# Attention scores as three 64-row products a head, gate arithmetic held behind attention, and higher ranks for evacuations and mLSTM steps

## The chip, the cores and the metric

One of the eight cores of a Trainium2 chip runs the whole program. The metric is the device time of one execution in microseconds (us), the median of several runs. The engines are TensorE (in the rows: PE for products, PEld for weight loads), VectorE (DVE), ScalarE (ACT), GpSimd (POOL) and SyncE (SP, which issues the DMAs).

## The reference

Two layers of a hybrid decoder over 1040 positions (16 learned meta tokens and 1024 inputs) of width 1024. Each layer normalizes its input, projects it once to 6408 columns, runs two groups of heads on the result, gates them, and projects back.

```
def hybrid_layer(x, ...):
    h = rms_norm(x, norm_g)
    z = h @ w_in
    aq, ak, av, ag, mq, mk, mv, mi, mf, mo, mgate = split(z)
    q, k = partial_rope(rms_norm(aq)), partial_rope(rms_norm(ak))     # 16 heads of 64, 2 kv heads
    ya = sliding_window_sink_attention(q, k, av, sink) * silu(ag)     # window 128, 16 meta keys, a sink
    qk = silu(causal_depthwise_conv([mq, mk]))                        # 4 mLSTM heads of 128
    hm = mlstm_chunkwise(mq, mk, mv, mi + b_i, log_sigmoid(mf + b_f)) # values of 256
    ym = rms_norm(hm) * sigmoid(mo) * silu(mgate)
    return x + concat(ya, ym) @ w_out
```

In attention, `scores = q k^T`; a query sees the meta keys, the keys of its window and a sink logit.

## The kernel before, in words

All arithmetic is float32. A matrix product is made of parts: each operand is split into a high part `hi`, rounded to the type that TensorE takes in one pass, and the rest `lo = x - hi`. A product is then `hi hi + hi lo + lo hi`, three passes into one PSUM bank. ScalarE makes `hi` (a copy), VectorE or GpSimd `lo` (a subtraction).

The 1040 positions stand as nine tiles, `TT`: one of 16 and eight of 128. A layer has these stages: keys and values; then attention; then the mLSTM; then the output projection (`pss`, `pj`, `po` at L1169).

**Attention.** Heads go in eight pairs `j`. For each pair and block `b` (nine blocks in the first layer, eight in the second, 136 steps in all) four tasks run: `s1` makes the scores of both heads in the two banks of a tile `S` and the softmax; `s2` transposes the probabilities into `T`, and evacuates them as `hi` and `lo` (L707 to L711); `s3` and `s4` multiply with the values into `O` and evacuate (L742, L744). `step(i)` emits `s1` of step i, `s2` of step i-2, `s3` and `s4` of step i-3. `weave` puts projections for coming stages between the steps, by parts of a few products (`projT_parts`, `projN_parts`, L224). TensorE's instructions keep the order of the program here (`pin`, while `in_order[0]` holds).

For the scores, `q_stacks` transposes a half pair of queries into a bank, and `q_put` splits it: for each head the 64 rows of `hi` and the 64 rows of `lo` stand one above the other in 128 rows. `Ks[0]` and `Ks[1]` hold `hi` and `lo` of the keys, each twice, in rows 0 to 63 and 64 to 127. So one product of 128 rows with `Ks[0]` gives `hi hi + lo hi`, a second with `Ks[1]` the rest: two products a head, four a step, of 272 columns (144 in the first full block of a pair, 16 in the block of the meta tokens).

**After attention** the TensorE order is free again, and the banks are given out anew. `gates` (L762 and on) computes the mLSTM's gate rows for all heads, first with Abs, Exp and Ln on ScalarE (L767 to L769); Ln needs a load of another function table. Its transposes (L772, L773) write a bank that attention used. Convolutions (`conv_tasks`, L854 to L862) run beside.

**The mLSTM.** For each of four heads `m_tasks` gives 27 steps and more: `sa(c)` prepares chunk `c` (splits of values and keys at L916, L917, L922, L923, products by `mm_split` at L904), `sb(c)` computes its result, `sc_(c)` transposes it. They are woven with projections for values (`v_tasks`), convolutions and output gates (`mo_tasks`).

Outside the pinned stretches, and for all engines but TensorE inside them, the order of an engine's instructions comes from a planner that replays the program with its own costs and takes the ready instruction of best rank first. The rank is the place in the program; `tc.high_priority(offset=EARLY)` moves it 80 places ahead, and -EARLY back. `tc.issue_after(x)` keeps instructions behind `x` on `x`'s engine. Weights come in by SP's DMAs, and are split into a ring of eight pairs by ScalarE (L158) and GpSimd (L159).

Of the kernel before, what the change touches and what calls it, by code (L numbers as in the profile page):

```python
# [15 lines left out]
ALU = mybir.AluOpType  # L16
# [46 lines left out]
def build(ctx, tc, I, O):  # L63
# [298 lines left out]
    for l in range(DEPTH):  # L362
# [9 lines left out]
        VR = unit()[:, :].rearrange("p (t c) -> p t c", t=9)  # L372
        KT = unit()[:, :].rearrange("p (a c) -> p a c", a=8)
        SS = []
        blk = [0, 0]

        def k_chain(kg, ta, tb):
# [214 lines left out]
            return [lambda i=i: st["post", half][i]() for i in range(4)]  # L592

        def q_put(Q, ps, n):
            Q = Q.rearrange("p (h c) -> p h c", h=2)
            sc.activation(Q[0:64, 0], ps[0:64, 0:n], AF.Copy)
            sc.activation(Q[64:128, 1], ps[64:128, 0:n], AF.Copy)
            ve.tensor_tensor(Q[64:128, 0], ps[0:64, 0:n], Q[0:64, 0], op=ALU.subtract)
            ve.tensor_tensor(Q[0:64, 1], ps[64:128, 0:n], Q[64:128, 1], op=ALU.subtract)  # L599

        def q_unit(j, g):
            if ("Q", g) not in A[j]:
# [46 lines left out]
        def att_tasks(j, st):  # L649
# [3 lines left out]
            def s1(b):  # L653
                t0, p = TT[b]
                S = SS[blk[0] % 2]
                blk[0] += 1
                k0, kn, o = (0, 16, 128) if b == 0 else (0, 144, 128) if b == 1 else (16 + (b - 2) * 144, 272, 0)
                for h in range(2):
                    U = st["Q", b > 4]
                    i = (b - 1) % 4  # L660
                    lq = U[:, 1024 + 16 * h:1040 + 16 * h] if b == 0 else U[:, 512 * h + 128 * i:512 * h + 128 * i + 128]
                    for i in range(2):
                        pin(pe.matmul(S[:p, h, o + 2 - 2 * h:o + 2 - 2 * h + kn], lq, Ks[i][:, k0:k0 + kn],
                                  start=(i == 0), stop=(i == 1)))
                if st.setdefault("S", 0) < 2:
                    ve.tensor_copy(cols(S, 1, 783, 1), snk[:, l, 2 * j:2 * j + 2].rearrange("p (h c) -> p h c", c=1))
                st["S"] += 1
                band = cols(S, 2, 654, 128)
                if b == 0:
                    ve.memset(band[:p], NEG)  # L670
                    mk = mask[:p, 128:144].bitcast(U32).rearrange("p (a c) -> p a c", a=1).to_broadcast([p, 2, 16])
                    ve.copy_predicated(cols(S, 130, 510, 16)[:p], mk,
                                       neg[:p].rearrange("p (a c) -> p a c", a=1).to_broadcast([p, 2, 16]))
                else:
                    if b == 1:
                        ve.memset(cols(S, 2, 510, 128), NEG)
                    ve.copy_predicated(band, mask.bitcast(U32).rearrange("p (h c) -> p h c", h=2),
                                       cols(S, 146, 366, 128))
                mx = sm.tile([128, 3, 2], F32, name="mx", bufs=4)
                P = tp_.tile([128, 384], F32, name="t")  # L680
                ve.tensor_reduce(mx[:p, 0], cols(S, 1, 639, 145)[:p], axis=mybir.AxisListType.X, op=ALU.max,  # L681
                                 negate=True)
                for h in range(2):
                    sc.activation(P[:p, 145 * h:145 * h + 145], S[:p, h, 1 + 127 * h:146 + 127 * h], AF.Exp,  # L684
                                  bias=mx[:p, 0, h:h + 1], accum_out=mx[:p, 1, h:h + 1])
                ve.reciprocal(mx[:p, 2], mx[:p, 1])  # L686
                for h in range(2):
                    Pn = P[:p, 1 + 144 * h:145 + 144 * h]
                    sc.activation(Pn, Pn, AF.Copy, scale=mx[:p, 2, h:h + 1])  # L689
                live[b] = P  # L690
# [39 lines left out]
            def s4(b):  # L730

                t0, p = TT[b]
                pm, OW, O = live.pop(b)
                G = st["G"]
                prods = [(VM[:, kv, h, :], pm[:, 0:p], O[:, p * h:p * h + p]) for h in range(2)]
                if b > 1:
                    prods += [(DV[:, b - 2], OW[:, c:c + 256], O) for c in (0, 256)]
                for i, (V, R, o) in enumerate(prods):
                    pin(pe.matmul(o, V, R, start=(b == 0), stop=(b == 0 or i == len(prods) - 1)))
                up, y = w1k(), w1k()  # L740
                with tc.high_priority(offset=EARLY):
                    sc.activation(up[0:64, 0:2 * p], O[64:128, 0:2 * p], AF.Copy)  # L742
                    for h in range(2):
                        ve.tensor_tensor(y[64 * h:64 * h + 64, :p], O[0:64, p * h:p * h + p],  # L744
                                         up[0:64, p * h:p * h + p], op=ALU.add)
                    if "QM" in st:
                        q_put(q_unit(j + 1, 0)[:, 1024:1056], st.pop("QM"), 16)
                gp.tensor_tensor(G[:, t0:t0 + p], G[:, t0:t0 + p], y[:, 0:p], op=ALU.mult)  # L748
                for t0, n, tiles in CH:
                    if b == tiles[-1]:  # L750
                        a = N_META if (t0 == 0 and last) else t0
                        sy.dma_start(spool[j, :, a:t0 + n], G[:, a:t0 + n])
# [9 lines left out]
        def gates(GR):  # L762
# [1 line left out]
            li = GT[:, 0].rearrange("p t h -> p (t h)")  # L764
            e = sm.tile([128, NR], F32, name="ge")
            lf = sm.tile([128, NR], F32, name="glf")
            sc.activation(e, zf, AF.Abs)  # L767
            sc.activation(e, e, AF.Exp, scale=-1.0)
            sc.activation(e, e, AF.Ln, bias=1.0)  # L769
            ve.scalar_tensor_tensor(lf, zf, 0.0, e, ALU.min, ALU.subtract)  # L770
# [51 lines left out]
        def v_tasks(h, wgf, st):  # L822
            def tile_task(t):
                p = TT[t][1]
                if t == 0:
                    v_units(st)
                ps = projN(wgf(), t, 256)
                sc.activation(st["V"](t)[:p, 0:256], ps[:p, 0:256], AF.Copy)
            return [lambda t=t: tile_task(t) for t in range(9)]

        def v_parts(h, wgf, st):
# [11 lines left out]
        def conv_tasks(h, wgf, st):  # L843
            def chunk_task(which, c):
# [6 lines left out]
                out, RAW = st["qk"[which]], st["raw"]  # L851
                t0, n, _ = CH[c]
                ps = projT(wgf(), 128 * which, t0, n)
                sc.activation(RAW[:, 3 + t0:3 + t0 + n], ps[:, :n], AF.Copy)  # L854
                z = t384(n)
                ve.tensor_scalar(z, RAW[:, t0:t0 + n], wcol(0), cw[:, l, 32 + tj:33 + tj],
                                 ALU.mult, ALU.add)
# [7 lines left out]
        def mo_tasks(u, wgf, st, held=None):  # L865
            def chunk_task(c):
                a, n, _ = CH[c]
                e = a + n
                a = N_META if (c == 0 and last) else a
                n = e - a  # L870
                ps = projT(wgf(), 0, a, n)
                t1 = t384(n)
                sc.activation(t1, ps[:, :n], AF.Tanh, scale=0.5)  # L873
                ps = projT(wgf(), 128, a, n)
                t2 = t384(n)
                sc.activation(t2, ps[:, :n], AF.Tanh, scale=0.5)  # L876
                ve.scalar_tensor_tensor(t2, t2, 1.0, ps[:, :n], ALU.add, ALU.mult)  # L877
                if held is None:
                    ve.scalar_tensor_tensor(t1, t1, 1.0, t2, ALU.add, ALU.mult)
                    gate_store(8 + u, st["Y"][u % 2], t1, a, e)  # L880
                    return
                if c == 0:
                    st["G", u] = unit()
                t3 = st["G", u][:, a:e]
                ve.scalar_tensor_tensor(t3, t1, 1.0, t2, ALU.add, ALU.mult)
                held.append(lambda: gate_store(8 + u, st["Y"][u % 2], t3, a, e))
            return [lambda c=c: chunk_task(c) for c in range(3)]

        def m_tasks(h, st):
# [11 lines left out]

            def mm_split(out, a, b):
                for i, (x, y) in enumerate(((a[0], b[0]), (a[0], b[1]), (a[1], b[0]))):
                    pin(pe.matmul(out, x, y, start=(i == 0), stop=(i == 2)))  # L904

            def sa(c):
                t0, p = TT[c]
# [9 lines left out]
                gp.tensor_tensor(V[1], v, V[0], op=ALU.subtract)  # L917
                if c < 8:
                    pk = bank("pt")
                    pin(pe.transpose(pk[:p, 0:128], kc, ident))  # L920
                    kt = KQ[:p, 0:128], KQ[:p, 128:256]
                    sc.activation(kt[0], pk[:p, 0:128], AF.Copy, scale=TK[:p, 2, r:r + 1])  # L922
                    ve.scalar_tensor_tensor(kt[1], pk[:p, 0:128], TK[:p, 2, r:r + 1], kt[0],  # L923
# [13 lines left out]
                De = w1k()  # L937
                sc.activation(De[:p, :p], st["EB"][:p, c, :p], AF.Exp, bias=TK[:p, 3, r:r + 1])
                pS = bank("pss")
                pin(pe.matmul(pS[:p, :p], kc, qc, start=True, stop=True))  # L940
                ve.tensor_tensor(De[:p, :p], pS[:p, :p], De[:p, :p], op=ALU.mult)
                DR = w1k(F32R)
                dr_ = DR[:p, 0:p], DR[:p, 128:128 + p]
# [39 lines left out]
            def sc_(c):  # L983
# [3 lines left out]
                hs = live.pop(c)  # L987
                ph = bank("pt")
                for f in range(2):
                    pin(pe.transpose(ph[:, 128 * f:128 * f + p], hs[:p, 128 * f:128 * f + 128], ident[:p, :p]))  # L990
                for f in range(2):
                    u = 2 * h + f
                    sc.activation(st["Y"][f][:, t0:t0 + p], ph[:, 128 * f:128 * f + p], AF.Copy,
                                  scale=cw[:, l, 40 + u:41 + u])

            out = [begin]
            for c in range(11):
                if c < 9:
                    out.append(lambda c=c: sa(c))
                if 0 <= c - 1 < 9:  # L1000
                    out.append(lambda c=c - 1: sb(c))
                if 0 <= c - 2 < 9:
                    out.append(lambda c=c - 2: sc_(c))
            return out


# [262 lines left out]
```

## Time and profile before

| what | value |
|---|---|
| median of 3 runs | 1961.46 us (1961.37 to 1962.85) |
| the profiled execution, its own time | 1962.62 us |
| its span, first to last instruction | 1960.9 us |
| TensorE products, busy | 1912.5 us (98%) |
| TensorE weight loads, busy | 1801.3 us (92%) |
| VectorE, ScalarE, GpSimd, busy | 1095.6, 1062.0, 915.8 us |
| mean granted TensorE clock | 0.997 of full speed |

Busy time of TensorE runs from a product's issue to its modelled end, and products overlap in the pipeline: what one product adds to a dense stream is the distance from its start to the next start. Layer 1 has its attention from about 76 to 415 us and its mLSTM to about 815; layer 2 from about 1045 to 1384 and to 1775.

### The profile page before, as it was taken

What the parts mean: (1) busy time and instruction counts of PE and PEld (TensorE: products, weight loads), DVE (VectorE), ACT (ScalarE), POOL (GpSimd) and SP (SyncE); (2) the same over time, 40 slices, a digit from 0 to 9 for tenths busy, and PEclk for the clock granted to TensorE, in tenths of its full rate; (3) what the DMA queues carried; (4) which work ended last, traced back from release to release, by engine and by line L of the source; (5) the groups of instructions that cost most, each with busy time, mean ns of one, the idle gap of its engine ahead of it and who ended that gap; (6) DMA issues with size and microseconds to landing.
All of it is one profiled execution on the core that took longest, in us unless ns stands there. A gap on an engine that the chain in (4) does not pass through costs nothing. (4 is left out here: it accounts for less than half of the span.)

```text
span 1960.9 us, 36174 instructions
## 1 busy us (share of the span) xinstructions
PE 1912.5 (98%) x12827; PEld 1801.3 (92%) x12827; DVE 1095.6 (56%) x2962; ACT 1062.0 (54%) x3133; POOL 915.8 (47%) x1106
## 2 busy tenths in 40 slices
PE   8999999999999999999999999999999999999999
PEld 7998998989999999877889999999999999998787
DVE  7777777667445363432446678776673635436211
ACT  6677777746454544643334677777364535446221
POOL 3544544336545454654335345443364454646342
PEclk9999999999999999999999999999999999999999
DMA  4111111121222121454541111112122121216543
GB/s 152 44 37 51 39 40 34 36 64 38 58 58 60 41 56 56 147 180 153 170 132 49 40 36 54 43 37 59 39 59 63 40 67 49 57 52 193 170 143 128
DMA packets 150838, 148.28 MB, mean 76 GB/s; under 512 B 15081, under 2 KB 123921, under 8 KB 150658
## 3 DMA queue, kind: packets, MB, share of 16 engines
q1 hardware_dynamic: 150658, 145.97, 25.5%
q8 instruction: 101, 1.65, 0.4%
q14 instruction: 79, 0.65, 0.1%
HBM read 122.58 MB, written 23.29 MB: 74 GB/s over the span
## 5 line engine op out<-in xcount | busy, mean ns | idle before, releaser
L184 PE MATMUL pj<-H,RING 128*128 128x384 f32 (+2 forms) x3456 | 578.5, 323 | 0.3 <-ACT t L873 0.3
L184 PEld LDWEIGHTS pj<-H,RING 128*128 128x128 f32 x3456 | 546.2, 189 | 2.8 <-issue 0.7
L159 POOL TENSOR_TENSOR RING<-raw,RING 128x512 fp32r<-128x512 f32 (+1 forms) x196 | 260.2, 1335 | 135.8 <-ACT RING L158 119.2
L224 PE MATMUL pj<-RING,H 128*128 128x256 f32 (+1 forms) x1920 | 268.2, 286 | 2.3 <-DVE u L636 2.3
L224 PEld LDWEIGHTS pj<-RING,H 128*128 128x128 f32 x1920 | 242.5, 189 | 2.7 <-DVE u L636 2.5
L224 PE MATMUL pj<-H,RING 128*128 128x384 f32 (+2 forms) x1152 | 216.2, 326 | 4.0 <-DVE u L599 4.0
L176 POOL TENSOR_TENSOR RING<-raw,RING 128x512 fp32r<-128x512 f32 x96 | 125.8, 1316 | 178.9 <-ACT RING L175 162.9
L184 PE MATMUL pj<-RING,H 128*128 128x256 f32 x1536 | 202.9, 287 | 3.3 <-DVE H L297 1.1
L184 PEld LDWEIGHTS pj<-RING,H 128*128 128x128 f32 x1536 | 190.7, 191 | 6.1 <-DVE H L297 1.7
L224 PEld LDWEIGHTS pj<-H,RING 128*128 128x128 f32 x1152 | 179.4, 189 | 4.9 <-PE T L703 2.3
L175 ACT ACTIVATE RING<-raw 128x512 fp32r<-128x512 f32 x128 | 80.8, 632 | 181.2 <-DMA raw<-in_w_out_dram 165.8
L158 ACT ACTIVATE RING<-raw 128x512 fp32r<-128x512 f32 (+1 forms) x196 | 122.5, 629 | 70.2 <-DMA raw<-in_w_in_dram 53.0
L748 POOL TENSOR_TENSOR u<-u,w1k 128x128 f32<-128x128 f32 (+1 forms) x136 | 64.4, 474 | 172.0 <-DVE w1k L744 166.3
L714 POOL TENSOR_SCALAR_AFFINE_SELECT p<-p 128x512 fp32r<-128x512 f32 x112 | 73.0, 652 | 128.9 <-DVE p L710 128.4
L684 ACT ACTIVATE t<-S,mx 128x145 f32<-128x145 f32 (+1 forms) x272 | 100.5, 374 | 59.8 <-DVE mx L681 56.4
L917 POOL TENSOR_TENSOR p<-u,p 128x258 fp32r<-128x258 f32 x64 | 46.7, 730 | 168.5 <-ACT p L916 168.4
L1169 PE MATMUL pss<-RING,H 128*128 128x512 f32 x384 | 120.5, 395 | 0.0
L859 DVE SCALAR_TENSOR_TENSOR t<-u,cw,t 128x384 f32<-128x384 f32 (+1 forms) x144 | 109.5, 760 | 2.6
L1169 PE MATMUL pj<-RING,H 128*128 128x512 f32 x352 | 109.8, 394 | 0.2 <-ACT H L1143 0.2
L689 ACT ACTIVATE t<-t,mx 128x144 f32<-128x144 f32 (+1 forms) x272 | 97.8, 407 | 19.2 <-DVE mx L686 19.1
L744 DVE TENSOR_TENSOR w1k<-O,w1k 64x128 f32<-64x128 f32 (+1 forms) x272 | 74.6, 274 | 37.8 <-ACT w1k L742 35.2
L877 DVE SCALAR_TENSOR_TENSOR t<-t,pj 128x384 f32<-128x384 f32 (+2 forms) x48 | 24.5, 510 | 125.7 <-ACT t L876 125.5
(343 smaller groups left out, 3809.3 us busy)
## 6 DMA issues: line engine op xcount, KB each, us to landing
raw<-in_w_out_dram SPq DMA_DIRECT2D x128, 256.0 KB, 2.8
raw<-in_w_in_dram SPq DMA_DIRECT2D x100, 256.0 KB, 2.8
raw<-in_w_in_dram SPq DMA_DIRECT2D x192, 128.0 KB, 2.3
spool<-u SPq DMA_DIRECT2D x56, 192.0 KB, 1.9
p<-x SPq DMA_DIRECT2D x24, 256.0 KB, 4.1
t<-spool SPq DMA_DIRECT2D x28, 192.0 KB, 3.7
p<-spool SPq DMA_DIRECT2D x28, 192.0 KB, 3.4
u<-em SPq DMA_DIRECT2D x8, 576.0 KB, 6.4
```

The source lines that it names most:

```text
L158: sc.activation(hi, raw[:, :, 0:o], AF.Copy)
L159: eng.tensor_tensor(lo, raw[:, :, 0:o], hi, op=ALU.subtract)
L175: sc.activation(hi, raw, AF.Copy)
L176: (ve if i > 8 and i % 2 else gp).tensor_tensor(lo, raw, hi, op=ALU.subtract)
L184: last = pin(pe.matmul(out, a, b, start=(i == 0), stop=(i == n - 1)))
L224: pin(pe.matmul(out(), x, y, start=(k + i == 0), stop=(k == n - 1 and i == 2)))
L684: sc.activation(P[:p, 145 * h:145 * h + 145], S[:p, h, 1 + 127 * h:146 + 127 * h], AF.Exp, bias=mx[:p, 0, h:h + 1], accum_out=mx[:p, 1, h: ...
L689: sc.activation(Pn, Pn, AF.Copy, scale=mx[:p, 2, h:h + 1])
L714: gp.affine_select(OW, HL, [[0, 4], [1, 128]], ALU.is_ge, 0.0, base=0, channel_multiplier=-1)
L744: ve.tensor_tensor(y[64 * h:64 * h + 64, :p], O[0:64, p * h:p * h + p], up[0:64, p * h:p * h + p], op=ALU.add)
L859: ve.scalar_tensor_tensor(z, RAW[:, t0 + i:t0 + i + n], wcol(i), z, ALU.mult, ALU.add)
L1169: pin(pe.matmul(ps[:p, :], a, b, start=(i + n == 0), stop=(i == 15 and n == len(terms) - 1)))
```

## The change

The queries are no longer stacked: `q_put` writes `hi` of both heads in the first half of the unit (head 0 in rows 0 to 63, head 1 in rows 64 to 127), and `lo` of both in the second, one instruction for each. A score is the sum of three products of 64 rows, `hi hi`, `hi lo` and `lo hi`, and the products of the two heads take turns: six instructions a step where there were four. The heads write different banks of `S`, as before.

The first ScalarE instruction of `gates` is held behind the last evacuation of `O` in attention. The evacuations of projections in `v_tasks`, `conv_tasks` and `mo_tasks` get the rank EARLY. So do all steps `sa`, `sb`, `sc_` of the mLSTM, but their products and transposes on TensorE, which keep the rank that they had.

```
         def q_put(Q, ps, n):
-            Q = Q.rearrange("p (h c) -> p h c", h=2)
-            sc.activation(Q[0:64, 0], ps[0:64, 0:n], AF.Copy)
-            sc.activation(Q[64:128, 1], ps[64:128, 0:n], AF.Copy)
-            ve.tensor_tensor(Q[64:128, 0], ps[0:64, 0:n], Q[0:64, 0], op=ALU.subtract)
-            ve.tensor_tensor(Q[0:64, 1], ps[64:128, 0:n], Q[64:128, 1], op=ALU.subtract)
+            sc.activation(Q[:, 0:n], ps[:, 0:n], AF.Copy)
+            ve.tensor_tensor(Q[:, n:2 * n], ps[:, 0:n], Q[:, 0:n], op=ALU.subtract)
...
-                for h in range(2):
-                    U = st["Q", b > 4]
-                    i = (b - 1) % 4
-                    lq = U[:, 1024 + 16 * h:1040 + 16 * h] if b == 0 else U[:, 512 * h + 128 * i:512 * h + 128 * i + 128]
-                    for i in range(2):
-                        pin(pe.matmul(S[:p, h, o + 2 - 2 * h:o + 2 - 2 * h + kn], lq, Ks[i][:, k0:k0 + kn],
-                                  start=(i == 0), stop=(i == 1)))
+                U = st["Q", b > 4]
+                i = (b - 1) % 4
+                qs = (U[:, 1024:1040], U[:, 1040:1056]) if b == 0 else (
+                    U[:, 128 * i:128 * i + 128], U[:, 512 + 128 * i:640 + 128 * i])
+                for n, (x, y) in enumerate(((0, 0), (0, 1), (1, 0))):
+                    for h in range(2):
+                        rows = slice(64 * h, 64 * h + 64)
+                        pin(pe.matmul(S[:p, h, o + 2 - 2 * h:o + 2 - 2 * h + kn], qs[x][rows], Ks[y][rows, k0:k0 + kn],
+                                      start=(n == 0), stop=(n == 2)))
...
-                    sc.activation(up[0:64, 0:2 * p], O[64:128, 0:2 * p], AF.Copy)
+                    att_end[0] = sc.activation(up[0:64, 0:2 * p], O[64:128, 0:2 * p], AF.Copy).ins
...
-            sc.activation(e, zf, AF.Abs)
+            with tc.issue_after(att_end[0]):
+                sc.activation(e, zf, AF.Abs)
...
                 ps = projN(wgf(), t, 256)
-                sc.activation(st["V"](t)[:p, 0:256], ps[:p, 0:256], AF.Copy)
+                with tc.high_priority(offset=EARLY):
+                    sc.activation(st["V"](t)[:p, 0:256], ps[:p, 0:256], AF.Copy)
...
-                    pin(pe.matmul(out, x, y, start=(i == 0), stop=(i == 2)))
+                    there(pe.matmul, out, x, y, start=(i == 0), stop=(i == 2))
+
+            def there(f, *a, **k):
+                with tc.high_priority(offset=-EARLY):
+                    pin(f(*a, **k))
...
+            def ranked(f, c):
+                with tc.high_priority(offset=EARLY):
+                    f(c)
+
             out = [begin]
             for c in range(11):
                 if c < 9:
-                    out.append(lambda c=c: sa(c))
+                    out.append(lambda c=c: ranked(sa, c))
...
```

The evacuations in `conv_tasks` (L854) and `mo_tasks` (L873, L876, L877) are put under `tc.high_priority(offset=EARLY)` as that in `v_tasks` is, `sb` and `sc_` are put under `ranked` as `sa` is, and the other products and transposes of `m_tasks` go through `there`.

## Rows read from the trace of the kernel before

**Rows 1.** The page's first part: busy us, share of the span, instructions.

```profile
PE 1912.5 (98%) x12827; PEld 1801.3 (92%) x12827; DVE 1095.6 (56%) x2962; ACT 1062.0 (54%) x3133; POOL 915.8 (47%) x1106
```

**Rows 2.** Busy us of each engine (instructions), granted clock, DMA share, GB/s, by stretch.

```profile
76.00:396.00 320.00, 305.27 (x2337) 296.56 (x2336) 229.86 (x694) 231.76 (x787) 141.50 (x194) 0.99 0.15 41
440.00:800.00 360.00, 358.55 (x2500) 353.09 (x2499) 184.13 (x533) 184.82 (x551) 189.74 (x243) 1.00 0.20 53
```

**Rows 3.** Waits of TensorE, whole span: for whom, us in total, times, longest us.

```profile
PE T L700 <- DVE ptm L711: 7.5, 5, 3.1
PE O L727 <- DVE w1k L744: 6.0, 8, 1.7
PE pj L224 <- DVE u L599: 4.0, 5, 1.1
PE S L663 <- ACT t L684: 3.1, 2, 2.1
PE O L727 <- DVE u L599: 2.6, 4, 1.1
...
PE pss L904 <- POOL p L917: 1.8, 2, 1.2
```

**Rows 4.** Timeline, TensorE's products: start us, us, line, output and inputs, shapes, count.

```profile
297.13 0.67 PE L663 MATMUL S<-u 128*128 128x272 f32 x4
297.64 1.24 PE L224 MATMUL pj<-RING,H 128*128 128x256 f32 x9
```

**Rows 5.** The same, around products of 16 rows in the mLSTM (16*128 is rows*weight columns).

```profile
720.84 0.85 PE L184 MATMUL pj<-H,RING 128*128 128x384 f32 x4
721.62 0.62 PE L904 MATMUL pss<-p,p 16*128 16x258 f32 x3
722.17 0.21 PE L940 MATMUL pss<-u 128*16 128x16 f32 x2
```

**Rows 6.** Timeline of weight loads in that place, the first alone and all three.

```profile
721.62 0.18 PEld L904 LDWEIGHTS pss<-p,p 16*128 16x128 f32 x1 [0.25 <-issue]
...
721.62 0.41 PEld L904 LDWEIGHTS pss<-p,p 16*128 16x128 f32 x3 [0.25 <-issue]
```

**Rows 7.** Timeline, TensorE's products, before one of 36 rows.

```profile
433.07 0.76 PE L184 MATMUL pj<-RING,H 128*128 128x256 f32 x5
433.76 0.25 PE L805 MATMUL po<-cst,u 36*128 36x36 f32 x1
```

**Rows 8.** Timeline, TensorE's products, before one of 96 rows.

```profile
47.96 1.01 PE L184 MATMUL pj<-RING,H 128*128 128x256 f32 x7
48.81 0.25 PE L354 MATMUL po<-cst,w1k 96*128 96x96 f32 x1
```

**Rows 9.** Groups by line and shape: count | busy us, mean ns | idle before, releasers.

```profile
L663 PE MATMUL S<-u 128*128 128x272 f32 x448 | 75.4, 290 | 4.4 <-ACT t L684 3.1 <-DVE u L598 0.9 <-DVE u L599 0.3
L599 DVE TENSOR_TENSOR u<-pj,u 64x512 fp32r<-64x512 f32 x30 | 20.8, 694 | 0.5
L568 ACT ACTIVATE u<-pj 128x512 f32<-128x512 f32 x32 | 19.1, 596 | 13.8 <-PE pj L224 13.7
L597 ACT ACTIVATE u<-pj 64x512 fp32r<-64x512 f32 x30 | 17.8, 594 | 0.5
```

**Rows 10.** Timeline of ScalarE at the end of the first layer's attention.

```profile
397.87 1.28 ACT L769 ACT_TABLE_LOAD   x1
...
400.24 0.38 ACT L707 ACTIVATE p<-T 128x256 fp32r<-128x256 f32 x1
```

**Rows 11.** Timeline of TensorE there, and at the same place of layer 2.

```profile
402.21 0.27 PE L700 MATMUL T<-cst,t 128*32 128x128 f32 x1 [3.06 <-DVE ptm L711]
...
1371.08 0.27 PE L700 MATMUL T<-cst,t 128*32 128x128 f32 x1 [2.52 <-DVE ptm L711]
```

**Rows 12.** Busy times by stretch after these two waits; the clock stands after POOL.

```profile
402.20:408.20 6.00, 5.99 (x27) 6.00 (x28) 3.25 (x8) 2.25 (x4) 1.71 (x4) 0.72 0.17 44
1371.00:1377.00 6.00, 5.92 (x27) 5.95 (x28) 3.33 (x8) 2.25 (x4) 1.79 (x4) 0.72 0.19 46
```

More of the change, by code (lines that the diff above doesn't have):

```diff
@@ L374, in build @@
         SS = []
+        att_end = [None]
         blk = [0, 0]
@@ L853, in chunk_task @@
                 ps = projT(wgf(), 128 * which, t0, n)
-                sc.activation(RAW[:, 3 + t0:3 + t0 + n], ps[:, :n], AF.Copy)
+                with tc.high_priority(offset=EARLY):
+                    sc.activation(RAW[:, 3 + t0:3 + t0 + n], ps[:, :n], AF.Copy)
                 z = t384(n)
@@ L872, in chunk_task @@
                 t1 = t384(n)
-                sc.activation(t1, ps[:, :n], AF.Tanh, scale=0.5)
+                with tc.high_priority(offset=EARLY):
+                    sc.activation(t1, ps[:, :n], AF.Tanh, scale=0.5)
                 ps = projT(wgf(), 128, a, n)
                 t2 = t384(n)
-                sc.activation(t2, ps[:, :n], AF.Tanh, scale=0.5)
-                ve.scalar_tensor_tensor(t2, t2, 1.0, ps[:, :n], ALU.add, ALU.mult)
+                with tc.high_priority(offset=EARLY):
+                    sc.activation(t2, ps[:, :n], AF.Tanh, scale=0.5)
+                    ve.scalar_tensor_tensor(t2, t2, 1.0, ps[:, :n], ALU.add, ALU.mult)
                 if held is None:
@@ L919, in sa @@
                     pk = bank("pt")
-                    pin(pe.transpose(pk[:p, 0:128], kc, ident))
+                    there(pe.transpose, pk[:p, 0:128], kc, ident)
                     kt = KQ[:p, 0:128], KQ[:p, 128:256]
@@ L939, in sa @@
                 pS = bank("pss")
-                pin(pe.matmul(pS[:p, :p], kc, qc, start=True, stop=True))
+                there(pe.matmul, pS[:p, :p], kc, qc, start=True, stop=True)
                 ve.tensor_tensor(De[:p, :p], pS[:p, :p], De[:p, :p], op=ALU.mult)
@@ L989, in sc_ @@
                 for f in range(2):
-                    pin(pe.transpose(ph[:, 128 * f:128 * f + p], hs[:p, 128 * f:128 * f + 128], ident[:p, :p]))
+                    there(pe.transpose, ph[:, 128 * f:128 * f + p], hs[:p, 128 * f:128 * f + 128], ident[:p, :p])
                 for f in range(2):
@@ L994, in sc_ @@
                                   scale=cw[:, l, 40 + u:41 + u])
+            def ranked(f, c):
+                with tc.high_priority(offset=EARLY):
+                    f(c)
             out = [begin]
@@ L998, in m_tasks @@
                 if c < 9:
-                    out.append(lambda c=c: sa(c))
+                    out.append(lambda c=c: ranked(sa, c))
                 if 0 <= c - 1 < 9:
-                    out.append(lambda c=c - 1: sb(c))
+                    out.append(lambda c=c - 1: ranked(sb, c))
                 if 0 <= c - 2 < 9:
-                    out.append(lambda c=c - 2: sc_(c))
+                    out.append(lambda c=c - 2: ranked(sc_, c))
             return out
```

## The prediction

> **What bounds the kernel now.** I read the busy times first [rows 1]. TensorE is busy 98% of the span, and each other engine little more than half of it. That figure alone doesn't prove a bound, since a product that waits in the pipeline counts as busy. So next comes the table by stage [rows 2]: in one attention stage TensorE is busy 305.3 of 320 us, in the mLSTM stage 358.6 of 360. Then the waits of TensorE alone [rows 3]: the reader should see that they are many, short (3.1 us at most) and nearly all ended by VectorE or ScalarE in attention. The stage of the mLSTM has hardly any: products of L904 waited 1.8 us for GpSimd's split (L917), in all of the kernel. So a change pays in full what it adds to TensorE's products, and can win back only these waits.
>
> What a product takes is read from starts, not from durations, which overlap. The four score products start at 297.13 and the next projection product at 297.64 [rows 4]: 0.51 us, so 0.125 us each, at 272 columns. A weight load of 128 columns with nothing in its way is followed by the next 0.11 us later (three loads of 0.18 us take 0.41 us, so (0.41 - 0.18) / 2 [rows 6]), which the 0.125 us just covers.
>
> **The change part by part.**
>
> *Scores, the number of products.* 448 products of 272 columns [rows 9] are 112 steps of four; 16 more steps of four have 144 columns, 8 have 16 (one head pair, one block each). Now each step has six products of 64 rows, in three pairs, heads in turn. The trace has no two products on different rows. Bounds: six at 0.125 us one after the other are 0.75 us; if the two of a pair run together, as two halves of the 128 rows that one product feeds today, it is 3 x 0.125 = 0.375 us, less than today's 0.50. The nearest row for a pair that covers all 128 rows is the full product [rows 4], so I take 0.375 us.
>
> *Scores, going from 128 rows to 64 and back.* Here the trace speaks. Four products of 384 columns run from 720.84, 0.17 us apart, so the slot of the last ends at 721.52. The next product, of 16 rows, starts only at 721.62, and its weight load with it [rows 5, 6]: 0.10 us in which the array empties, then a load of 0.11 us with nothing to cover it. After three products (3 x 0.12 us) the next of 128 rows starts at 722.17, another 0.08 us late, again with a bare load, 0.11 us at 128 columns. Together 0.10 + 0.11 + 0.08 + 0.11 = 0.40 us for going and coming back. A product of 36 rows pays the same: five products from 433.07, 0.12 us apart, end their slots at 433.67, and it starts at 433.76 [rows 7]. One of 96 rows pays nothing: seven products from 47.96, 0.122 us apart, end their slots at 48.81, and there it starts [rows 8]. 64 rows could be of either kind; they use half the array, as 36 would if rounded up to halves, and 96 can't be cut that way. I take 0.40 us. The Trainium skill, TensorEngine Tiling (Array Packing), Key Properties, says that changing the tiling mode drains TensorE, and lists 64 rows as a mode of its own; that these rows show a gap at 16 and 36 rows agrees with it, and no row here has 64.
>
> The step of 272 columns: 0.40 + 0.375 - 0.50 = +0.275 us, x 112 = +30.8 us. With 144 columns four products are paced by their loads, 4 x 0.11 = 0.44: 0.40 + 0.33 - 0.44 = +0.29, x 16 = +4.6. The eight of 16 columns pay the changes alone, some 0.25 each, as they stand before 16-row transposes that change anyway: +2. Sum +37 us (bounds below). No other work hides it: TensorE has no idle time but the waits.
>
> *q_put.* Two ScalarE copies and two VectorE subtractions of 64 x 512 become one of each of 128 x 512. A copy takes as long from 128 rows (L568, 0.596 us) as from 64 (L597, 0.594), so one copy of 0.59 and one subtraction of 0.69 us (L599) are saved per unit [rows 9], and the chain from the transposes to the free bank is about 1.2 us shorter. The waits ended by L599 come to 4.0 + 2.6 = 6.6 us, none over 1.1 [rows 3]: all can go. The other attention waits shown are 6.0 + 3.1, and of 7.5 for L711 some 1.9 that are not the gates': 11 us. With TensorE 6% slower a step and VectorE relieved, I let 7 of them and of smaller ones go (bounds 0 and 13). What is late next is the chain from S through VectorE (L744), at a smaller lag. Together -13.5 us.
>
> *Gates behind attention.* From 397.87 ScalarE stands 1.28 us in a table load (L769) while the copies out of T (L707) come due; they run at 400.24 [rows 10], and TensorE waits 3.06 us until 402.21, in the second layer 2.52 [rows 11]. For 6 us after each wait the mean granted clock is 0.72 [rows 12], so part of the stretch ran at 1.2 GHz instead of 2.4: 6 x 0.28 = 1.7 us lost, twice. With L767 to L769 behind the last copy out of O, the copies and subtractions out of T are still waited for, some 0.7 us. So 5.6 + 3.4 - 1.4 = 7.6 us come back. The gates now start some 19 us later, but their transposes (L772) stand behind the attention's banks in any case. Queued behind the held L767 are L768, L769, VectorE's L770 and those transposes, and on SP the store of em (L797), which weight loads follow. The cover is the conv projections, 24 products of 0.125 to 0.17 us each; if it is gone, the table load and the small steps, about 2 us a layer, are paid. Bounds -9 and +4; I take -7.5.
>
> *Ranks.* Copies, splits and small steps of the mLSTM go ahead of weight splits in ScalarE's, VectorE's and GpSimd's queues; products get their old rank back, and no DMA is moved by itself. At most 1.8 us of waits can go [rows 3]. Queued behind them is the weight split (L159) on GpSimd, and TensorE waits for that if it comes late; GpSimd is busy 190 of 360 us there [rows 2], so I expect none of it. Take -1.5, bounds -2 and +8.
>
> Sum: 37 - 13.5 - 7.5 - 1.5 = +14.5 us on the profiled execution's 1962.6 us (span 1960.9): 1977. The median of the runs is 1.2 us lower: **1976 us**. Its own range, from the bounds: 37 - 20 - 9 - 2 is +6, and 37 - 7 + 4 + 8 is +42, the latter only if all goes badly: 1964 to 1990.
>
> **The rivals.**
>
> *Loads one at a time.* The products of a pair run together, but the six loads follow one another as bare ones do, 0.11 us each [rows 6]. A pair then takes 0.22 us: 0.40 + 0.66 - 0.50 = +0.56 x 112 = 63; 16 x (0.40 + 0.66 - 0.44) = 10; +2: +75, and with 18 instead of 13.5 us of waits gone +48: 2009. For it: in no row do two loads start closer than that. Against it: those all go to the same rows. Chance 0.27.
>
> *Nothing runs together.* Six at 0.125: (0.40 + 0.75 - 0.50) x 112 = 73, +10 + 2 = 85, less 27: 2019. The 16-row products, all on the same rows, keep 0.12 us apart [rows 5], which is for it. Chance 0.14. The Trainium skill, TensorE: Matmul & The Clock Gate, The mechanism, has products on different row groups start some 4 ns apart and overlap. By that, this rival would fall and the sum above stand; no row of this trace shows it.
>
> *The other side: no change of mode at 64 rows*, as at 96, and pairs together: (0.375 - 0.50) x 112 = -14, -2 for the steps of 144 columns, and -20 from the other parts: 1926 us. The point from which it decides: the other parts bring 22.5 us, or 0.165 us a step over 136 steps, so going and coming must cost under 0.125 + 0.165 = 0.29 us. Rows 7 speak against it, rows 8 for it. Chance 0.08.
>
> **How the numbers follow.** The forecast has 0.48, the three rivals 0.27, 0.14 and 0.08, and 0.03 is left for ranks or gates that cost ten us or more. What a measurement tells from no change here is 0.2%, or 1957.5 to 1965.4. The forecast's low edge, where all waits go, gives 0.07 of "same" and 0.02 of faster; with the last rival, faster is 0.10. Slower has 0.83. The range reaches from 1960 to 2020: about 0.1 is left out below, 0.07 above.
>
> **What would show it.** Score groups: the first load of each starts about 0.1 us after the slot before it and the next projection product 0.1 us late; pairs start within some ns of each other (right), 0.11 us apart (loads), or 0.125 (nothing together); from the first score product's start to the next projection product's about 0.11 + 0.375 + 0.08 = 0.57 us, 0.85 or 0.94. TensorE's waits that the subtraction of `q_put` ends come to near nothing. At the end of attention no table load between copies out of T, and no low clock there. In the mLSTM stage no new waits for RING. The prediction is wrong if there is no gap at the scores, or if attention's waits grow because the scores' pairs hold both banks of S longer.

## The result and the profile after

The changed kernel takes 1967.17 us (median of 11 runs, 1966.23 to 1972.18) where the kernel before takes 1961.54 on the same chip (11 runs, 1959.73 to 1964.0): a ratio of 1.0028, 95% interval 1.002 to 1.0036. It is slower by 5.6 us. The direction is the one forecast and the time lies in the range that was stated, 1964 to 1990. The forecast of 14.5 us more was too large by 9, and 5.6 is just under the +6 that its own lower bounds add up to. The profiled execution has 1967.73 us and a span of 1966.0, 5.1 more than the one before.

First the page's busy times of the kernel after, to be held against [rows 1]:

```profile
PE 1935.2 (98%) x13099; PEld 1789.1 (91%) x13099; DVE 1061.4 (54%) x2922; ACT 1045.2 (53%) x3093; POOL 912.1 (46%) x1106
```

TensorE has 272 products more, VectorE and ScalarE 40 instructions fewer each, and VectorE is relieved of 34 us, ScalarE of 17. Now a score group in the timeline of TensorE, products and then weight loads, at the place in the step of [rows 4]:

```profile
294.87 1.29 PE L224 MATMUL pj<-RING,H 128*128 128x256 f32 x9
296.09 0.64 PE L664 MATMUL S<-u 64*128 64x272 f32 x6
296.67 0.39 PE L224 MATMUL pj<-RING,H 128*128 128x256 f32 x1
...
296.09 0.42 PEld L664 LDWEIGHTS S<-u 64*128 64x128 f32 x6
296.67 0.19 PEld L224 LDWEIGHTS pj<-RING,H 128*128 128x128 f32 x1 [0.15 <-issue]
```

From the first score product to the next projection product it is 0.58 us; 0.57, 0.85 or 0.94 were forecast for pairs, for loads one at a time and for nothing together. That each pair runs together is seen by ending the window a little later each time. These are the products under way between 296.09 and 296.10, then up to 296.33, then up to 296.46:

```profile
296.09 0.39 PE L664 MATMUL S<-u 64*128 64x272 f32 x2
...
296.09 0.52 PE L664 MATMUL S<-u 64*128 64x272 f32 x4
...
296.09 0.64 PE L664 MATMUL S<-u 64*128 64x272 f32 x6
```

Two within 10 ns, the next two by 0.24, the last two by 0.37 us: three pairs, and from the recorded starts the partners lie mostly 3 to 4 ns apart, products and loads alike. The second pair starts 0.23 us after the first, the third 0.125 after the second and the next product 0.22 after that (medians), where full products are 0.125 apart: part of the price of the change of rows lies inside the group. The last load shown above has 0.15 us of nothing ahead of it, and the product of the next projection starts with it: the bare load on the way back to 128 rows. The Trainium skill, TensorE: Matmul & The Clock Gate, The mechanism, gives some 4 ns for products on different row groups; here the trace agrees, with 3 to 4 ns.

Then TensorE's waits over the whole span, the largest of those in attention and behind it (for whom, us in total, times, longest us), against [rows 3]:

```profile
PE T L701 <- DVE ptm L712: 3.2, 2, 1.7
PE O L728 <- DVE w1k L745: 2.5, 4, 1.3
...
PE pj L1183 <- ACT H L1157: 1.9, 1, 1.9
PE pss L1183 <- ACT H L1157: 1.9, 1, 1.9
...
PE S L664 <- ACT t L685: 1.6, 1, 1.6
PE po L792 <- DVE rw L789: 1.3, 1, 1.3
...
PE pj L184 <- DVE w1k L192: 0.9, 1, 0.9
```

The waits for `q_put`'s subtraction (L599, L598 after) are gone. Two waits for L712 (L711 before) are left, both at the end of attention, and there are new ones: for H at the start of both output projections, and for a late link of `gates` (L789).

Last the place of [rows 11, 12]: the wait behind attention in the first layer, and busy times with the granted clock (behind POOL's) in the two stretches of 6 us around and after it:

```profile
398.45 0.27 PE L701 MATMUL T<-cst,t 128*32 128x128 f32 x1 [1.69 <-DVE ptm L712]
```

```profile
398.00:404.00 6.00, 5.55 (x35) 5.58 (x36) 3.94 (x10) 1.77 (x6) 2.08 (x4) 1.00 0.27 68
404.00:410.00 6.00, 6.00 (x42) 6.00 (x41) 5.10 (x14) 1.96 (x6) 1.20 (x2) 1.00 0.01 3
```

The wait of 3.06 us has become 1.69 and the clock stays at 1.00, where it was 0.72. But two stretches at half of the full clock, 1.2 GHz, stand elsewhere. The first begins 1 us behind the wait of 1.9 us for H at the output projection of layer 1, the second is in the first steps of the second attention. Before there were three, the two of [rows 12] and the one of the last line below:

```profile
810.40:813.80 3.40, 3.17 (x9) 2.45 (x10) 3.17 (x11) 2.59 (x10) 1.85 (x3) 0.50 0.76 202
1073.20:1076.60 3.40, 3.40 (x14) 2.79 (x12) 2.57 (x10) 2.89 (x13) 0.00 (x0) 0.50 0.28 80
...
239.00:242.40 3.40, 3.40 (x17) 3.40 (x17) 1.30 (x5) 2.50 (x8) 3.40 (x5) 0.50 0.46 137
```

**Where the time went.** The stages, between starts of products on TensorE, in us:

```
stage                                    before   after   difference
to the first score, layer 1                77.1    77.0   -0.1
attention, first to last score, layer 1   314.5   312.1   -2.4
rest of attention, layer 1                 22.5    19.75  -2.7
mLSTM, layer 1                            401.05  400.6   -0.4
output projection, layer 1                203.0   204.8   +1.8
to the first score, layer 2                52.45   52.3   -0.2
attention, first to last score, layer 2   290.4   300.3   +9.9
rest of attention, layer 2                 21.95   19.55  -2.4
mLSTM, layer 2                            393.2   393.9   +0.7
output projection and end                 184.8   185.7   +0.9
```

The two attentions are not alike: one got shorter. The slots around the 136 score groups tell how that goes together. A slot runs from a start to the next start; the columns are the slot ahead of the first score product, the way from that product to the first start behind the group, and the slot of the product behind it, each summed over all groups, in us, waits within included. The kernels from the third line on are those of the experiments:

```
kernel                          ahead   group   behind    sum
before                           22.7    69.0     18.7   110.4
after                            32.6    73.6     27.8   134.0
heads one after the other        32.1    74.6     27.9   134.6
four products of 128 rows        21.8    66.8     18.6   107.2
six products of 128 rows         20.2    96.6     18.4   135.2
three products of 128 rows       21.6    49.1     18.6    89.3
scores right before transposes   32.4    76.8     17.0   126.2
two blocks together (72 groups)  17.4    67.6      9.8    94.8
```

The scores cost 23.6 us more by that. All other slots of the two attentions sum to 13.0 and 2.5 us less than before, and nearly all of that is in slots of over 0.45 us, in which TensorE stood (15.3 to 2.8, and 6.9 to 2.4 us). So the change costs TensorE nearly what it should, and a large part comes back as time that TensorE no longer stands, in the first layer above all.

### The profile page after: what moved, and what is told of

Read it like the earlier page. It is cut to its first block, busy times and chain, and to the rows that moved or that the text cites. A ratio compares the mean times of both kernels' runs of the same rounds, so it can differ in the third digit from the quotient of the medians.

```text
span 1966.0 us, 36582 instructions
## 1 busy us (share of the span) xinstructions
PE 1935.2 (98%) x13099; PEld 1789.1 (91%) x13099; DVE 1061.4 (54%) x2922; ACT 1045.2 (53%) x3093; POOL 912.1 (46%) x1106
## 3 DMA queue, kind: packets, MB, share of 16 engines
q8 instruction: 103, 1.69, 0.4%
## 4 chain that ended last, share of the span: by engine, by line
PE 83%; DVE 4%; DMA 4%; POOL 3%; issue 3%; ACT 2%; SPq 0%; POOLq 0%; ACTq 0%; DVEq 0%
PE pj L184 33%; PE pj L224 18%; PE pss L1183 6%; PE pj L1183 5%; PE po L1183 5%; PE S L664 3%; PE O L740 2%; PE po L914 2%; PE pss L914 2%; DMA raw<-in_w_in_dram 2%; PE O L728 2%; POOL RING L159 2%; PE T L704 1%; PE pt L914 1%; PE pj L208 1%
## 5 line engine op out<-in xcount | busy, mean ns | idle before, releaser
L184 PE MATMUL pj<-H,RING 128*128 128x384 f32 (+2 forms) x3456 | 584.2, 322 | 0.1
L224 PE MATMUL pj<-RING,H 128*128 128x256 f32 (+1 forms) x1920 | 272.9, 288 | 0.0
L224 PE MATMUL pj<-H,RING 128*128 128x384 f32 (+2 forms) x1152 | 220.7, 330 | 0.0
L184 PE MATMUL pj<-RING,H 128*128 128x256 f32 x1536 | 209.1, 287 | 3.7 <-DVE H L297 1.6
L685 ACT ACTIVATE t<-S,mx 128x145 f32<-128x145 f32 (+1 forms) x272 | 99.9, 371 | 65.4 <-DVE mx L682 64.5
L690 ACT ACTIVATE t<-t,mx 128x144 f32<-128x144 f32 (+1 forms) x272 | 97.8, 406 | 14.1 <-DVE mx L687 13.8
L745 DVE TENSOR_TENSOR w1k<-O,w1k 64x128 f32<-64x128 f32 (+1 forms) x272 | 74.6, 274 | 47.5 <-ACT w1k L743 45.1
```

What stands on the lines that cost most here:

```text
L184: last = pin(pe.matmul(out, a, b, start=(i == 0), stop=(i == n - 1)))
L224: pin(pe.matmul(out(), x, y, start=(k + i == 0), stop=(k == n - 1 and i == 2)))
```

## The experiments

Theory 1 is the mechanism of the prediction: going to 64 rows and back empties TensorE and leaves loads bare, the pairs run together, and a shorter chain through `q_put` gives waits back. Theory 2, in the later runs, is the same with the prices that the slots gave (0.09 us ahead of a group, 0.11 behind) and ranks that are worth nothing. The rival of each run stands in its expectation. Ratios are to the kernel before on the same chip.

**Scores and q_put alone** (the kernel before with the new `q_put` and the new products, no edit at gates or ranks):

> The kernel before with the new q_put and the new score products alone; gates and ranks as before. Theory 1 (the score groups cost TensorE about 32 us, of which some 24 us of attention waits come back; the gates' order returns 5 to 7 us more; the ranks are about nothing): 1961.5 + 32 - 24 = 1970 to 1974 us, with the waits and the low clock at the end of attention as before. Rival (the ranks or the gates hide part of the scores' price): over 1976 us, with attention waits not gone. Rival (the gates' order returns nothing): 1967 us, as the changed kernel.

Measured: 1967.04 us, ratio 1.0038 (1.0025 to 1.0051), or 7.5 us more (4.9 to 10.0). Theory 1 had 8.5 to 12.5 more and the rival, by which the gates return nothing, 5.5; the interval leaves both open. All of the loss is in this part, and it is a third of the 37 - 13.5 = 23.5 us that the prediction has for it.

**Gates and ranks alone** (the kernel after with the old `q_put` and the old four products):

> The changed kernel with q_put and score products as before: gates and ranks alone. Theory 1: 1961.5 - 5 to -7 = 1954.5 to 1957 us, no low clock at the end of attention. Rival (the waits there only move): 1960 to 1962 us.

Measured: 1956.35 us, ratio 0.9985 (0.9977 to 0.9994), about 3 us less, where 9 were forecast for the two and 5 to 7 were expected here: neither theory 1 nor the rival.

**Gates alone** (the kernel before with this edit):

```
...
-            sc.activation(e, zf, AF.Abs)
+            with tc.issue_after(att_end[0]):
+                sc.activation(e, zf, AF.Abs)
```

> The kernel before with the gates' first instruction held behind attention, nothing else. Theory 1, by which the ranks add nothing or cost one to two us at the end of the mLSTM (a wait of 1.9 us for the split of the first output operand in each layer): one to two us under the run with gates and ranks, 1953 to 1956. Rival (the ranks bring the gain): 1960 to 1962.

Measured: ratio 0.9992 (0.9983 to 1.0), 1956.98 us, which can't be told from the run with both. **Ranks alone** (the second experiment without that edit):

> The kernel before with the ranks alone. Theory 2: within 2 us of the kernel before, with the waits for L1157 at the end of the mLSTM and without those for L968 and L917. Rival (the ranks gain): 3 us or more under it.

Measured: 1960.41 us, ratio 1.0006 (0.9997 to 1.0015): nothing that can be told from no change. The waits for L917 and L968 go from 3.9 us to 1.8 in its trace, not to nothing; two of 1.7 and 1.8 us for the split of the first output operand (L1157 in the kernel after) come at the output projections, and one of 1.6 in the mLSTM. What the waits don't show is the clock: in each of the ten traces of kernels with the ranks, one output projection or both begin with a stretch of 3.4 us at a granted clock of 0.50, within 2.1 us of their first product, and in none of the four without (before, scores and q_put alone, gates alone, two blocks without the ranks).

**Heads one after the other.** Six products as in the change, but three of head 0, then three of head 1:

```
-                for n, (x, y) in enumerate(((0, 0), (0, 1), (1, 0))):
-                    for h in range(2):
+                for h in range(2):
+                    for n, (x, y) in enumerate(((0, 0), (0, 1), (1, 0))):
```

> The changed kernel with the three products of head 0 first and then the three of head 1, all else the same. Theory 1, by which products overlap only with a neighbour on other rows: one overlap of a possible three is left, so a group of 272 columns takes 5 x 0.125 instead of 3 x 0.125 us, +0.25 x 112 + 0.22 x 16 = +31.5 us, less some waits: 1990 to 1998 us. Rival (the engine pulls the other head's products ahead whatever the order): 1967 us.

Measured: 1965.91 us, ratio 1.0033 (1.0019 to 1.0046). What I held of the order fell. Its timeline of products, ended at 296.215, 296.225 and 296.45 us:

```profile
296.21 0.39 PE L664 MATMUL S<-u 64*128 64x272 f32 x1
...
296.21 0.40 PE L664 MATMUL S<-u 64*128 64x272 f32 x2
...
296.21 0.52 PE L664 MATMUL S<-u 64*128 64x272 f32 x4
```

Three pairs again, the partners some 10 ns apart by their recorded starts. The built program has the three of head 0 ahead of the three of head 1; the records don't say which product is which, but score products of 272 columns on the same rows never start less than 0.119 us apart in the kernel before (0.125 in the median). By that spacing the partner is the first on the other rows, the fourth of the program, and it doesn't stand behind the second and third. "In turn" is not what makes them overlap.

**q_put in four.** The kernel after, with `q_put` on 64 rows at a time, as before, but into the new places:

```
-            sc.activation(Q[:, 0:n], ps[:, 0:n], AF.Copy)
-            ve.tensor_tensor(Q[:, n:2 * n], ps[:, 0:n], Q[:, 0:n], op=ALU.subtract)
+            for a in (0, 64):
+                sc.activation(Q[a:a + 64, 0:n], ps[a:a + 64, 0:n], AF.Copy)
+            for a in (0, 64):
+                ve.tensor_tensor(Q[a:a + 64, n:2 * n], ps[a:a + 64, 0:n], Q[a:a + 64, 0:n], op=ALU.subtract)
```

> The changed kernel with the split of the queries in four instructions of 64 rows, as long as before, to the new places. Theory 1 (the shorter split gives back the waits that it ended, 6.6 us and more): 3 to 8 us above the changed kernel, 1970 to 1975, with TensorE waiting for the second subtraction again. Rival (the slack that slower scores give is enough by itself): 1967 to 1968, no such waits.

Measured: 1983.13 us, ratio 1.01 (1.0081 to 1.012). Against the 1.0028 of the kernel after that is 0.72%, some 14 us, for a saving that was put at less than half (3 to 8 us): more than theory 1 had, and not the rival. The waits of the first layer's attention (77 to 389 us) in it:

```profile
PE pj L224 <- DVE u L637: 3.6, 3, 1.4
PE pj L224 <- DVE u L600: 2.2, 2, 1.1
PE O L730 <- ACT RING L158: 1.9, 1, 1.9
```

The waits for the subtraction (L600) are back, and the waits around it too.

**The new q_put with the four products of 128 rows of before:**

> Gates, ranks and the new q_put in two instructions, but the four score products of 128 rows of the kernel before, which then mix the heads: the scores are not those of the reference, the work of every engine but for q_put is that of the run with gates and ranks. Theory 1: 6 to 9 us under that run, as the waits for the split go though TensorE is no slower. Rival (waits go only through TensorE's slack): the time of that run.

Measured: 1942.62 us, ratio 0.99 (0.9884 to 0.9916). Against gates and ranks alone (0.9985), from which it differs in `q_put` only, that is 0.85% or 16.7 us, where 6 to 9 were expected. And against the kernel after, which differs in the products only, it is 1.28%, 25 us: the net price of the new products. The waits of its first attention (77 to 389 us):

```profile
PE O L726 <- DVE w1k L743: 2.5, 3, 1.5
PE pj L224 <- DVE u L635: 1.6, 1, 1.6
PE T L699 <- DVE ptm L710: 1.0, 1, 1.0
```

**Six products of 128 rows**, and **three**, so that no product changes the rows:

> The changed kernel with each of the six score products taken over all 128 rows: same order, same banks, no change of rows on TensorE, and scores that mix the heads. Theory 1 (a pair overlaps, and going to 64 rows and back costs nearly all that this saves): group 6 x 0.125 = 0.75 us against 0.57 plus 0.09 ahead and up to 0.11 behind: the time of the changed kernel within 3 us. Rival (the change of rows costs less than read, the loss is elsewhere): 10 us or more above the changed kernel.

> The changed kernel with three products of 128 rows a step, one for head 0 and two for head 1: half of the score products are left out, and what is left mixes the heads. It stands for pairs that overlap with no change of rows. Theory 1: the group takes 0.375 us with nothing ahead or behind, 0.36 us less a step, x 136 = -48 us, less waits that come up again (10 to 18): 1929 to 1937 us. Rival (TensorE's time at the scores isn't what bounds attention): above 1945 us.

Measured: 1970.21 us, ratio 1.0037 (1.0023 to 1.0051), and 1933.42 us, 0.9851 (0.9834 to 0.9867). In the table of slots six full products have nothing extra ahead or behind, and 23 us more within the group. Three full products stand for three pairs that overlap with no change of rows. By them, overlapping saves (135.2 - 89.3) / 136 = 0.34 us a group, and the change of rows takes (134.0 - 89.3) / 136 = 0.33: the two are alike at three pairs. A group of 272 columns ahead of a projection pays 0.092 + (0.573 - 0.377) + 0.106 = 0.39 us by the medians, where the prediction took 0.40. And with three products of 128 rows, the same stream without a change of rows, the kernel would be 29 us faster than before, not 6 slower.

**Scores right before the transposes.** In the slots, the product behind a group is late by 0.106 us (median) where it is a projection, but only by 0.012 where it is a transpose with 32 columns of weights (L701). So every group was put before those:

```
-                out.append(lambda: s1(b))
+                b0, put = (steps[i - 2][1], steps[i - 2][3]) if i >= 2 else (0, None)
+                out.append(lambda: (s1(b), put and put(b0)))
...
```

> The changed kernel with the transposes of step i-2 put directly behind the scores of step i, no projection products between. Theory 2 (a change of rows costs 0.09 us ahead, a bare load and an emptying inside the group, and 0.11 us behind when a full weight load follows, but 0.01 when a load of 32 columns does): some 83 of 136 groups save 0.06 to 0.1 us, -8 us against the changed kernel, 1958 to 1961. Rival (the moved transposes come before their softmax is done, and wait): 1965 to 1970, with new waits at the transposes.

Measured: 1967.61 us, ratio 1.0047 (1.0034 to 1.0059): nothing won. The slots did shrink by 8 us, but other waits came: for `q_put`'s subtraction (L598) and the evacuation of O (L745) at the products into O, and for the softmax (L690) at the transposes, which were moved ahead. Its waits from 77 to 389 us, and the largest from 1068 to 1366 us:

```profile
PE O L728 <- DVE u L598: 1.8, 3, 0.9
PE O L728 <- DVE w1k L745: 1.6, 6, 0.5
PE T L701 <- ACT t L690: 1.4, 2, 0.9
...
PE O L728 <- DVE w1k L745: 5.1, 6, 1.8
```

**Scores of two blocks together**, so that the rows change half as often, with all three parts of the change, and then without the ranks:

```
...
+                if after:
+                    out[-1] = lambda: (s1(b), s1(b + 1), put and put(b0))
...
```

> The changed kernel with the scores of two blocks emitted together, once every two steps, and the transposes of step i-2 directly behind: 72 groups of 64-row products instead of 136. Theory 2: each of 64 groups joined saves an emptying ahead and behind and a bare load, 0.355 us, and 0.06 for what follows: -22 to -26 us, less waits that come up as TensorE is faster: 1942 to 1950 us. Rival (two softmaxes come at once, ScalarE and VectorE are late for S and T): above 1957, with new waits for L685 or the copies out of T.

> The same with the ranks of evacuations and mLSTM steps as before the change, gates held as in it. Theory 2, by which the ranks trade waits of 1 us for others of 1.9 (first output operand, L1157): 0 to 3 us under the run with two blocks. Rival (the ranks help the mLSTM stage): 2 us or more above it.

Measured: 1970.65 us, ratio 1.0054 (1.0041 to 1.0067), and 1971.77 us, 1.0074 (1.0059 to 1.0088). Theory 2 had the second at or under the first; it is above it, as the rival had it, but the intervals overlap. The scores give back 39 us of TensorE's time (134.0 to 94.8 in the table), a group of twelve takes 0.96 us:

```profile
293.70 1.02 PE L664 MATMUL S<-u 64*128 64x272 f32 x12
294.66 0.29 PE L701 MATMUL T<-cst,t 128*32 128x128 f32 x1
```

and all of it is lost again. The largest waits from 77 to 389 us, where the kernel after has 2.0 us in all, and from 1066 to 1366, where it has 2.7:

```profile
PE O L728 <- DVE w1k L745: 3.2, 3, 1.5
PE S L664 <- ACT t L685: 3.1, 3, 1.3
PE O L617 <- DVE w1k L745: 2.0, 3, 1.0
...
PE O L728 <- ACT ptm L709: 4.0, 2, 2.4
PE O L728 <- DVE w1k L745: 2.3, 3, 1.2
```

All listed waits of the two stretches come to 15.3 and 10.1 us, 20.7 more than after. They are mostly those that the rival named, for the softmax's reading of S (L685) and the copies out of T (L709), beside the evacuation of O (L745): two steps' softmax come due at once. That the chain through ScalarE and VectorE sets the pace is inferred from them. Attention and its rest together are 4.5 us longer than after in the two layers, although the scores give back 39, so some 44 us are lost. The listed waits are 21 of them; the other 23 I haven't traced to single waits.

## Why the prediction was right in direction and too high

**Scores, +37: right in mechanism, measured +31.5.** The median slot ahead of a group is 0.092 us longer than before (0.10 was taken), a group of 272 columns takes 0.573 us from first start to the next start (0.501 before; 0.57 was forecast), one of 144 columns 0.486 (0.401), of 16 columns 0.166 (0.106). Behind it the next slot is 0.106 us longer with a projection. Over all groups: 136 x 0.092 = 12.5 ahead; 112 x 0.072 + 16 x 0.085 + 8 x 0.060 = 9.9 within; behind, 27.8 - 18.7 = 9.1 from the table. The sum is 31.5. The term was too large because the way back was charged alike everywhere, while 33 of the 128 full groups stand before the short loads of L701 and pay 0.012, seven 0.056 before transposes with 128 columns. The eight groups of 16 columns stand before projections, not before transposes of 16 rows, and pay about 0.02 behind. The Trainium skill, TensorEngine Tiling (Array Packing), Key Properties, has the drain at a change of mode that the prediction cited; the trace agrees at 64 rows: 0.09 us ahead of a group in the median, and none with six products of 128 rows.

**Rivals.** Loads one at a time and nothing together fell with the starts 3 to 4 ns apart; no change of mode fell with the slots ahead and behind. That it would have made the kernel faster is borne out: three products of 128 rows, whose slots need no change, are at 0.9851 or 29 us less, where the rival had 35 less.

**The waits of attention, "together -13.5": this step failed by size.** This is the step that made the forecast too high: "I let 7 of them and of smaller ones go" beside the 6.6 us of the subtraction, and, ahead of it, that a change "can win back only these waits". Attention from first to last score is 2.4 us shorter and 9.9 longer, 7.5 more in sum, with 31.5 more on TensorE: 24 us came back, where 13.5 were taken. Outside its bounds, too: with all waits gone the prediction allowed 20.

The list of waits explains part of it. The prediction read the largest rows of the whole span only; the waits of the two attention windows (77 to 389 and 1068 to 1361 us) together are 22.7 us (14.6 and 8.1) before, with two for L636 (2.3) and one for L708 (0.8) among them, and 4.7 after. That is 18. The rest, some 6 us, stands in no wait: the slots of over 0.45 us and those at the scores shrank by more than the waits listed. Up to half of it is how a wait is listed: it begins at the modelled end of the product ahead, 0.29 us after its start [rows 9], and not at the end of its slot of 0.125. There are 19 waits fewer (26 to 7), so up to 19 x 0.165 = 3.1 us are missing from the list, by estimate. The other 3 us I can't put to single causes.

The price of `q_put` itself was the larger error. A copy and a subtraction saved per unit were counted as the waits that L599 ended (6.6 us), where taking them away is worth 16.7 us with the old products and 14 with the new ones. With that edit alone (four products of 128 rows against gates and ranks) the listed waits of the two windows fall from 22.1 to 11.1 us: 7.0 were for the subtraction, 4.0 were named by other lines (2.3 of it L685), and 5.7 us of the gain stand in no listed wait. So a shorter copy and subtraction also brought what stood behind them forward; by which chain is not shown. The remaining 7 us of the 24 fit the slack that slower scores leave: with `q_put` in four, 31.5 us more of TensorE's time less the 3 us of gates and ranks make a kernel 20 us slower, not 28.5, so 9 us come back without the shorter split.

**Gates, "I take -7.5": right at its place, half lost again.** The rest of attention is 2.7 and 2.4 us shorter, and the low clock is gone there, as said. But 1.7 and 1.5 us of the wait stay where 0.7 was put, and behind the hold a new wait came, 1.3 us for L789 (those for L192 are 0.9 us in all, 0.8 before). Gates alone are worth 0.0008 of the time, 1.6 us, with an interval that touches none.

**Ranks, -1.5: nothing measurable.** Its bound of 1.8 us left out 2.1 for L968. The waits went (L917) or shrank (L968, to 0.5), but 1.9 us for H came at each output projection, which are 1.8 and 0.9 us longer, and 3.4 us at the half clock in the first, or some 1.7 us lost (3.4 x 0.5, an estimate). No new waits for RING in the mLSTM, as expected.

Sum by the runs: scores and `q_put` alone +7.5 where +23.5 was forecast, gates and ranks together -3 where -9 was forecast: +4.5, against 5.6 measured. The errors of the terms are -5.5 (scores), -10.5 (waits) and +6 (gates and ranks); that the last has the other sign, and so keeps the total in the range, is luck.

## What to carry to other kernels

A wait is named by the instruction that came last, and a lateness can stand in no list: of the 16.7 us that a shorter evacuation was worth, 7.0 stood under its own name. To price one, take the whole list of its stage and ask what stands behind it on both engines, or run a kernel that has only that edit. Two products on halves of the rows run as one, but going there and back cost about as much as the overlap brings for three pairs, so longer runs of pairs are needed, and a chain on the other engines that can take them. With the order of the steps kept, time saved on TensorE stays saved in the main: against the kernel after, four products of 128 rows save 26.8 us in the table of slots and 25 us of the time, three save 44.7 and 35. The 8 us and 39 us that another order of the steps saved turned into waits: it brought transposes or two softmaxes due before the other engines were done.

## What the runs showed of the hardware beyond that

Products on the two halves of the rows do not keep the order of the program among each other: with three of one head first, a product still starts 10 ns behind the first of all, which by the spacing on equal rows is the other head's. The Trainium skill, TensorE: Matmul & The Clock Gate, The mechanism, has products keep the program's order in start and end, and only weight loads overlap ahead of it; the starts of this run, 10 ns apart, differ from it. The way back to 128 rows depends on what comes next: behind a group of 272 columns a projection of 256 columns, with a load of 128 columns, is 0.106 us late, a transpose with a load of 128 columns 0.056, one with a load of 32 columns 0.012.
